# A channel shuffle: fewer, longer tiles, permuted inside one slot

## The chip, the core and the metric

The kernel runs on one core of a Trainium2 chip. The metric is the device time of one execution in microseconds (us); a lower time is better. Engines named here: VectorE (DVE in the profile) copies and rearranges data inside the on-chip memory SBUF; SyncE (SP) and ScalarE (ACT) do nothing here but issue DMAs; 16 DMA engines move data between HBM and SBUF. SBUF has 128 partitions, and sizes "a partition" are bytes in each of them.

## The reference

The input is an image batch of 16 x 64 x 64 pixels with 256 float32 channels each. The channels of every pixel are seen as 8 groups of 32 and are transposed to 32 rows of 8: the output channel j*8 + g is the input channel g*32 + j. No arithmetic is done.

```python
def reference(x, groups):
    batch, h, w, c = x.shape                       # 16, 64, 64, 256
    channels_per_group = c // groups               # 32
    x = x.reshape(batch, h, w, groups, channels_per_group)
    x = x.transpose(0, 1, 2, 4, 3)
    return x.reshape(batch, h, w, c).astype(np.float32)
```

The batch holds 65,536 pixels of 1 KB: 67.11 MB are read and 67.11 MB are written, at least once each.

## The kernel before

The pixels are taken in order. A piece of q pixels a partition is 128 x q consecutive pixels: partition p gets q consecutive pixels, q KB that lie in one run in HBM (`rows`, line 39). `_SLOTS` (line 12) lists the pieces: a first tile with pieces of 4 and 8 pixels, a tile of 28, twelve tiles of 38, and one of 16, together 512 pixels a partition. So there are 16 loads, 16 copies and 16 stores.

Each tile has an input buffer from a pool of two (`in_pool`) and an output buffer from a pool of three (`out_pool`), each as large as the largest tile, 38 KB a partition: 190 KB in all. For every piece three instructions are issued:

- line 55: SP issues the load into the input tile;
- line 57: VectorE copies the piece from the input tile to the output tile, reading with channels in the order (j, g) and writing in one run, which is the permutation;
- line 61: ACT issues the store of the output tile.

The order of instructions on each engine is the program's order (`manual_schedule`), and the waits between engines come from the tiles: a copy waits for its load and for a free output buffer, a store waits for its copy, a load waits until its input buffer has been read by the copy of two tiles before. Loads go through the one queue of SP (q1 in the profile) and stores through the one queue of ACT (q10). Both queues run on the same 16 DMA engines; each DMA of 128 partitions gives every engine eight rows, one packet each.

Of the kernel before, what the change touches and what calls it, by code (L numbers as in the profile page):

```python
# [1 line left out]

# [4 lines left out]


F32 = mybir.dt.float32
P = 128  # L10

_SLOTS = [[4, 8], [28]] + [[38]] * 12 + [[16]]
_IN_BUFS = 2
_OUT_BUFS = 3


@with_exitstack
def kernel(
    ctx: ExitStack,
    tc: tile.TileContext,  # L20
    x: bass.AP,
    groups: bass.AP,
    out: bass.AP,
):
    nc = tc.nc
    b, h, w, c = x.shape
    G = int(groups)
    CPG = c // G
    assert G * CPG == c
    assert sum(map(sum, _SLOTS)) * P == b * h * w  # L30
    biggest = max(map(sum, _SLOTS))

    x_flat = x.rearrange("b h w c -> (b h w c)")
    out_flat = out.rearrange("b h w c -> (b h w c)")

    in_pool = ctx.enter_context(tc.tile_pool(name="in_pool", bufs=_IN_BUFS))
    out_pool = ctx.enter_context(tc.tile_pool(name="out_pool", bufs=_OUT_BUFS))

    def rows(flat, first, q):

        return flat[first * c : (first + P * q) * c].rearrange("(p f) -> p f", p=P)

    ctx.enter_context(tc.manual_schedule(engines=None))
    first = 0
    for parts in _SLOTS:
        in_tile = in_pool.tile([P, biggest * c], F32, name="in_tile")
        out_tile = out_pool.tile([P, biggest * c], F32, name="out_tile")
        at = 0
        pieces = []
        for q in parts:  # L50
            pieces.append((q, first, slice(at * c, (at + q) * c)))
            first += P * q
            at += q
        for q, start, cols in pieces:
            nc.sync.dma_start(out=in_tile[:, cols], in_=rows(x_flat, start, q))  # L55
        for q, start, cols in pieces:
            nc.vector.tensor_copy(  # L57
                out=out_tile[:, cols].rearrange("p (i j g) -> p i j g", j=CPG, g=G),
                in_=in_tile[:, cols].rearrange("p (i g j) -> p i j g", g=G, j=CPG),
            )  # L60
            nc.scalar.dma_start(
                out=rows(out_flat, start, q), in_=out_tile[:, cols]
            )


# [1 line left out]
_INS = ['x', 'groups']  # L67
_OUTS = [((16, 64, 64, 256), 'float32')]

_NUMBERS = {'groups': 8}  # L70


# [26 lines left out]
```

## Time and profile before

| what | value |
|---|---|
| median of 3 runs | 316.04 us (316.04 to 316.05) |
| span of the profiled execution (first to last instruction) | 314.4 us |
| median less that span (no other time of the profiled execution is listed) | 1.6 us |
| DMA, mean over the span | 427 GB/s |
| VectorE busy | 119.0 us, 38%, 16 copies |
| data packets on each of the two queues | 2048, and 256 completions |

The profile is of one execution. Its 40 slices give the busy share of an engine in tenths, for DMA the mean share of the 16 DMA engines. "Chain that ended last" is followed back from the last instruction, step by step, to what released it. In the groups, the number after the bar is the group's busy time, then the mean duration of one instruction in nanoseconds, then the idle time of the engine before them and what ended it. In the windows, the columns are the stretch and its length, the busy time of VectorE and of GpSimd with their instruction counts, a clock that does not matter here, the busy share of the DMA engines and the GB/s that they moved. In a short window this rate is rough, since a packet of 38 KB on each of 16 engines is 0.62 MB.

### The profile page before, as it was taken

Reading aid. Unit: us, or ns where it says so; the run is one execution under the profiler, and the core shown is the slowest. Engines: PE = TensorE matmul, PEld = TensorE weight load, DVE = VectorE, ACT = ScalarE, POOL = GpSimd, SP = SyncE. Lnnn points to the kernel's source line nnn. Section 1 sums busy time; section 2 is a strip of 40 time slices with the busy share of each in tenths; the row PEclk is TensorE's granted clock in tenths of the full one; section 3 lists DMA queues with packets and bytes.
Section 4 is the critical chain, followed back from the end, with each engine's and each line's share of the span. In section 5 each row is a group of like instructions: output and inputs, shape, how many; then the busy total and the mean of one; then the engine's idle time right before and its main releaser. Section 6 shows DMA issues by size and latency. Waiting matters only on the chain.

```text
span 314.4 us, 132 instructions
## 1 busy us (share of the span) xinstructions
DVE 119.0 (38%) x16; POOL 0.2 (0%) x4
## 2 busy tenths in 40 slices
DVE  2081907309109109019028028037046055065400
POOL 0000000000000000000000000000000000000000
DMA  7999999999999999999999999999999999999997
GB/s 317 405 441 416 435 416 483 401 465 406 450 421 446 426 436 436 401 470 396 475 396 475 396 470 401 470 401 470 401 450 421 446 426 436 436 417 450 429 421 321
DMA packets 4608, 134.22 MB, mean 427 GB/s; under 512 B 512, under 2 KB 512, under 8 KB 768
## 3 DMA queue, kind: packets, MB, share of 16 engines
q1 hardware_dynamic: 2304, 67.11, 49.8%
q10 hardware_dynamic: 2304, 67.11, 49.4%
HBM read 67.11 MB, written 67.11 MB: 427 GB/s over the span
## 4 chain that ended last, share of the span: by engine, by line
DMA 76%; DVE 19%; issue 0%; SPq 0%; DVEq 0%
DMA in_tile<-in_x_dram 76%; DVE out_tile L57 19%; SPq L55 0%; DVEq L57 0%
## 5 line engine op out<-in xcount | busy, mean ns | idle before, releaser
L57 DVE COPY out_tile<-in_tile 128x9728 f32<-128x9728 f32 (+4 forms) x16 | 119.0, 7440 | 179.4 <-DMA in_tile<-in_x_dram 179.4
L80 POOL MEMSET const-uint8-127<- 128x1 uint8 x1 | 0.1, 103 | 0.0
L80 POOL MEMSET const-bfloat16-1.0<- 128x1 bf16 x1 | 0.1, 102 | 0.0
L80 POOL MEMSET const-float32-1.0<- 128x1 f32 x1 | 0.1, 100 | 0.0
L80 POOL MEMSET const-float32-0.0<- 128x1 f32 x1 | 0.1, 99 | 0.2 <-issue 0.2
## 6 DMA issues: line engine op xcount, KB each, us to landing
in_tile<-in_x_dram SPq DMA_DIRECT2D x12, 4864.0 KB, 37.0
out_dram<-out_tile ACTq DMA_DIRECT2D x12, 4864.0 KB, 42.6
in_tile<-in_x_dram SPq DMA_DIRECT2D x1, 3584.0 KB, 14.7
out_dram<-out_tile ACTq DMA_DIRECT2D x1, 3584.0 KB, 30.9
in_tile<-in_x_dram SPq DMA_DIRECT2D x1, 2048.0 KB, 30.4
out_dram<-out_tile ACTq DMA_DIRECT2D x1, 2048.0 KB, 15.2
in_tile<-in_x_dram SPq DMA_DIRECT2D x1, 1024.0 KB, 5.4
out_dram<-out_tile ACTq DMA_DIRECT2D x1, 1024.0 KB, 25.0
```

Source lines behind the costliest of these rows:

```text
L57: nc.vector.tensor_copy(out=out_tile[:, cols].rearrange("p (i j g) -> p i j g", j=CPG, g=G), in_=in_tile[:, cols].rearrange("p (i g j) -> ...
L80: nc = _bacc.Bacc("TRN2", target_bir_lowering=False, num_devices=1)
```

## The change

The twelve tiles become eleven of 43 pixels a partition and one of 39. There is one pool of four slots in place of the two pools, and a slot has room for 43 + 8 pixels, 51 KB a partition, 204 KB in all. A load puts its q pixels eight pixels (`_SHIFT`) above the place from which they will be stored. VectorE then permutes them inside the slot, eight pixels at a time, each piece written eight pixels below where it was read, so that a piece overwrites pixels that the piece before it has already read and moved. A tile of 43 takes six copies, the last of 3 pixels; the tile of 39 takes five, the last of 7: 71 copies in all. The store takes the lower q pixels of the slot and follows all of its tile's copies. A load now waits until the store of four tiles before has read the slot. There are 12 loads and 12 stores.

```diff
-_SLOTS = [[4, 8], [28]] + [[38]] * 12 + [[16]]
-_IN_BUFS = 2
-_OUT_BUFS = 3
+_SLOTS = [[43]] * 11 + [[39]]
+_BUFS = 4
+
+_SHIFT = 8
...
-    biggest = max(map(sum, _SLOTS))
+    room = max(map(sum, _SLOTS)) + _SHIFT
...
-    in_pool = ctx.enter_context(tc.tile_pool(name="in_pool", bufs=_IN_BUFS))
-    out_pool = ctx.enter_context(tc.tile_pool(name="out_pool", bufs=_OUT_BUFS))
+    pool = ctx.enter_context(tc.tile_pool(name="pool", bufs=_BUFS))
...
-        in_tile = in_pool.tile([P, biggest * c], F32, name="in_tile")
-        out_tile = out_pool.tile([P, biggest * c], F32, name="out_tile")
+        slot = pool.tile([P, room * c], F32, name="slot")
...
-            pieces.append((q, first, slice(at * c, (at + q) * c)))
+            pieces.append((q, first, at))
...
-        for q, start, cols in pieces:
-            nc.sync.dma_start(out=in_tile[:, cols], in_=rows(x_flat, start, q))
-        for q, start, cols in pieces:
-            nc.vector.tensor_copy(
-                out=out_tile[:, cols].rearrange("p (i j g) -> p i j g", j=CPG, g=G),
-                in_=in_tile[:, cols].rearrange("p (i g j) -> p i j g", g=G, j=CPG),
+        for q, start, at in pieces:
+            nc.sync.dma_start(
+                out=slot[:, (at + _SHIFT) * c : (at + _SHIFT + q) * c],
+                in_=rows(x_flat, start, q),
             )
+        for q, start, at in pieces:
+            for lo in range(at, at + q, _SHIFT):
+                n = min(_SHIFT, at + q - lo)
+                src = slot[:, (lo + _SHIFT) * c : (lo + _SHIFT + n) * c]
+                dst = slot[:, lo * c : (lo + n) * c]
+                nc.vector.tensor_copy(
+                    out=dst.rearrange("p (i j g) -> p i j g", j=CPG, g=G),
+                    in_=src.rearrange("p (i g j) -> p i j g", g=G, j=CPG),
+                )
             nc.scalar.dma_start(
-                out=rows(out_flat, start, q), in_=out_tile[:, cols]
+                out=rows(out_flat, start, q), in_=slot[:, at * c : (at + q) * c]
             )
```

## The prediction

> **What bounds the kernel now.** I read the page's busy times and 40 slices first, then the chain of waits, the groups with shapes kept apart, the waits of SP's queue, the windows, and last the trace's packet records (start, duration, queue and size of each DMA packet).
>
> ```profile
> span 314.4 us, 132 instructions
> ...
> DVE 119.0 (38%) x16; POOL 0.2 (0%) x4
> ...
> DMA  7999999999999999999999999999999999999997
> ...
> q1 hardware_dynamic: 2304, 67.11, 49.8%
> q10 hardware_dynamic: 2304, 67.11, 49.4%
> HBM read 67.11 MB, written 67.11 MB: 427 GB/s over the span
> ## 4 chain that ended last, share of the span: by engine, by line
> DMA 76%; DVE 19%; issue 0%; SPq 0%; DVEq 0%
> ```
>
> The 16 DMA engines are full in every slice but the first and the last: the two queues' shares add to 99.2%. The 19% of VectorE in the chain must not be read as a cost: the chain goes load, copy, load, but while it goes through a copy the store queue keeps the same 16 engines full.
>
> ```profile
> 0.00:2.00 2.00, 0.00 (x0) 0.20 (x4) 1.00 0.18 23
> ...
> 9.00:29.00 20.00, 6.57 (x1) 0.00 (x0) 1.00 1.00 423
> ...
> 60.00:260.00 200.00, 75.15 (x9) 0.00 (x0) 1.00 1.00 433
> ...
> 313.28:314.44 1.16, 0.00 (x0) 0.00 (x0) 1.00 0.00 0
> ```
>
> Last column GB/s: 23 in the first 2 us (the first packet starts at 1.75), 433 in the long mixed stage, 423 from 9 to 29 us, where loads take most of the turns, nothing in the last 1.16 us. VectorE's prices and what SP waits for:
>
> ```profile
> L57 DVE COPY out_tile<-in_tile 128x9728 f32<-128x9728 f32 x12 | 105.5, 8791 | 158.5 <-DMA in_tile<-in_x_dram 158.5
> ...
> L57 DVE COPY out_tile<-in_tile 128x2048 f32<-128x2048 f32 x1 | 2.0, 2019 | 1.5 <-DMA in_tile<-in_x_dram 1.5
> L57 DVE COPY out_tile<-in_tile 128x1024 f32<-128x1024 f32 x1 | 1.1, 1092 | 4.1 <-DMA in_tile<-in_x_dram 4.1
> ```
> ```profile
> SPq L55 <- DMA in_tile<-in_x_dram: 151.2, 13, 13.8
> SPq L55 <- DVE out_tile L57: 106.2, 13, 8.9
> ```
>
> SP is two loads ahead at most and waits for VectorE's copy before the next; a load takes 37 us to land, so its queue holds work meanwhile.
>
> **The time as a sum.** The packet records show one row of one tile per packet, eight rows per DMA and engine. Usual durations: 4096 B 159 ns, 8192 B 309, 16384 B 611, 28672 B 1062, 38912 B 1439. The slope is (1439 - 159)/(38912 - 4096) = 0.03676 ns a byte, and about 8 ns stay over. Each engine moves 134.22/16 = 8.389 MB: 308.41 us. In the mixed stage, with packet bytes spread evenly over their durations, the rate is 433.5 GB/s, so packets of 38912 B follow each other every 38912 x 16/433.5 = 1436.2 ns, 5.6 ns above their 1430.6 of bytes: the fixed cost of a packet, the completions' share in it. There are 256 data packets an engine (32 DMAs of eight): 1.43 us. The first packet starts at 1.75 us and the last ends at 313.28 us, a stretch of 311.53. So 311.53 - 308.41 - 1.43 = 1.69 us are lost otherwise. The records place most of it; an excess is what packets took above the usual for their size, summed and divided by 16:
>
> ```
> excess per engine        us     what runs there
> before 3 us              0.29   first packets, up to 679 ns instead of 159
> 3 to 32 us               0.52   loads alone, then loads with small stores
> 32.9 us                  0.36   one load packet on each engine, 1794 instead of 1439
> after that               0.02   equal loads and stores, then stores alone
> ```
>
> The remaining 0.50 is latency before the first bytes and the engines' spread at the end (their last completions lie 0.4 us apart). Stores alone, 294.5 to 307 us, run at 433.5 GB/s, as fast as the mix. Loads alone do not: 417 GB/s from 3 to 9 us. The stretch is one profiled execution of 314.44 us span; the median of the runs is 316.04, 1.60 more, which I carry over unchanged.
>
> **The change part by part.** *Fewer, longer packets.* 12 loads and 12 stores are 24 x 8 = 192 packets an engine, 64 fewer: 64 x 5.6 ns = 0.36 us saved. Bytes are the same. A 44032 B packet should take 44032 x 0.03676 + 8 = 1627 ns. The Trainium skill's "DMA: Bandwidth & Descriptors" (section "Why small descriptors are slow (HBM only)") gives some three cycles per packet; at 850 MHz, the clock in its port figure, an estimate of 64 x 3.5 = 0.23 us, less than the trace's price.
>
> *The first store.* Now the first tile is 4 KB a partition, copied at 4.06 us, with its first store packet at 9.12. After: the tile lands at about 1.75 + 0.5 + 8 x 1.66 = 15.5, VectorE starts 0.4 later as now. Six pieces: five of 2048 elements at 2.02 and one of 768 at about 0.86 (the 1024 row, 0.9 ns an element), with some 0.06 between them: 11.3 us, to 27.2. Now the first store packet comes 4.0 us after its issue (5.19), that is three load packets of 1.06 and 0.9; with packets of 1.63 it is 5.8. So stores begin at about 33 us, and loads are alone from 3 to 33: 30 us instead of 6, and the load-heavy 9 to 32 us go. The DMA engines are never idle in it: four loads are issued at once, 4 x 13.1 = 52 us of work.
>
> *What loads alone cost* (L). Rows, as excess over the usual packet: 8192 B alone 1.9% (3 to 6 us), 28672 B alone 5.3% (6 to 9 us), both together 3.4%; 38912 B with small stores in between 2.1% (19 to 29 us). Bounds: 1% (half of the least row, for a row pitch that spreads better) and 8% (the one worst microsecond, 8 to 9 us, 399 GB/s against 433.5), so 0.3 to 2.4 us. I take 3% of 30 us, 0.9 us, between the row nearest in packet size (2.1%) and the one nearest in kind (3.4%). It replaces the 0.52 of before. The 0.36 at 32.9 us comes once while packet sizes change; I let it go, and keep it as part of the range.
>
> A rule speaks against the change here: the same page ("Where 436 GB/s comes from") has HBM limit transfers to and from SBUF to about 358 GB/s a core; 30 us at that rate would lose 5.2 us and give about 320. The trace disagrees: loads alone ran at 417.
>
> *SP's wait.* A load now waits for the store of four tiles before, where it waited for a copy. Behind it in SP's queue stand only later loads; VectorE would wait for them. When stores begin, loads are (33 - 2.3)/13.26 = 2.3 tiles ahead, and both queues then take equal turns, as in the mixed stage (loads 215.6, stores 217.9 GB/s). When store k ends, loads stand at k + 3.3 of k + 4 issued: 0.7 tile, some 18 us, still queued against 1 to 2 us until a new load's packets come. Cost nothing; cover 18 us.
>
> *VectorE in the slot.* 71 copies instead of 16: 11 x 11.3 + 10.2 = 134 us instead of 119, in 12 rounds of 26 us each. Hidden by the DMA of other slots; without cover each tile would cost its 11.3. A piece writes where the piece before it read, on one engine in order. No row shows copies inside one tile; below, no gain is possible as VectorE is not waited for by DMA; above, even 4 us a piece (double) is 24 us a tile, still under 26.
>
> *The end.* The last store now is 16 rows, ready 9.6 us before its turn (copy ends 298.4, first packet 307.99). After, when the last load's packets end, stores stand at 11.91 - 2.3 = 9.6 tiles: 0.4 + 1 tiles alone, 18 us, before the last store's turn. Its copies need 0.4 + 10.2 + 0.9 = 11.5 us: 6.5 us to spare. Stores alone run at the full rate, so nothing is lost. After the last packet 1.16 us remain as now.
>
> **Sum.** 308.41 + 192 x 5.6 ns = 1.08, + 0.29 + 0.50 at the ends, + 0.9: 311.18 against 311.53, 0.35 us less. 316.04 - 0.35 = 315.7 us. The 0.2% that a measurement can tell from no change is 0.63 us here, so this is no change.
>
> **Rivals.** *Loads alone cost 2% or less.* The sum then is 310.28 + L with L below 0.62: more than 0.63 us saved. For it: the row nearest in size, 2.1%. Against it: 5.3% with 28672 B alone. Its time is 314.8 (L = 0, the floor) to 315.4; at 1.5% it is 315.2. *Loads alone cost over 6.3%*, 1.89 us, a rate under 406 GB/s, from which the change is slower by more than 0.2%: one mechanism, the read side of HBM in the first 33 us. For it: 399 GB/s at 8 to 9 us and the rows' rise from 1.9 to 5.3%. Against it: 421 to 425 in later single microseconds of nothing but long loads. At 8% it is 2.4 us: 317.2. *VectorE becomes the bound at the end.* If the pieces wait for each other and a tile of 39 takes over 17 us instead of 10, the last store is late and each further microsecond counts in full; at 4 us a piece (19 to 20 us) it adds 3: 318.7. Against it: gaps of copies now are only from waiting for loads. *The change does nothing at all to DMA's order*: equal packets in both queues and full engines, the loads-alone cost as small as the packets' gain; that is my forecast's own case.
>
> **How the numbers follow.** Forecast (L from 2.1 to 6.3%) 0.50, with its own range 315.4 to 316.7; cheaper loads 0.27; costlier loads 0.17; VectorE at the end 0.03; something unseen that slows, such as long rows in the largest slots, 0.03. Faster 0.27, same 0.50, slower 0.23. The range goes from 315.0 (L = 0.2) to 317.0 (L = 2.2): below and above it about 0.08 each.
>
> **What would show it.** Slices of DMA at 9 throughout; the first store packet at about 33 us; a rate of about 420 GB/s before it, 433 to 434 after; 44032 B packets at 1627 ns in the mix; loads never missing from their queue; VectorE about 134 us with idle time for loads only; the last store's packets following the one before without a gap. The prediction is wrong if the rate before the first store is under 406 or near 433, if the load queue runs dry, if pieces take far over 2.02 us, or if the mixed rate of the longer rows is not that of 38912 B.

## The result and the profile after

The changed kernel takes 319.31 us (median of 6 runs, 317.49 to 321.16), against 316.08 for the kernel before in the same session. The ratio is 1.010, 95% interval 1.0066 to 1.0134: 1% slower, where no change (315.7, range 315.0 to 317.0) was forecast. The runs also scatter: 3.7 us between the fastest and the slowest, against 0.5 us before. The profiled run took 320.60 us with a span of 318.8, so 1.8 us lie outside the span. Ratios, here and below, leave out runs over 1.5% above the fastest of their kernel; only the two kernels with three slots had such runs, two of ten and one of ten.

The page of the changed kernel, its busy engines, slices, queues and chain:

```profile
span 318.8 us, 168 instructions
...
DVE 138.7 (44%) x71; POOL 0.2 (0%) x4
...
DMA  8999999999999999999999999999999999999895
...
q1 hardware_dynamic: 1728, 67.11, 49.4%
q10 hardware_dynamic: 1728, 67.11, 48.8%
q14 instruction: 1, 0.01, 0.0%
HBM read 67.11 MB, written 67.11 MB: 421 GB/s over the span
## 4 chain that ended last, share of the span: by engine, by line
DMA 68%; DVE 18%; another core or an unknown queue 9%; issue 0%; SPq 0%; DVEq 0%
```

DMA is still the bound, but the mean rate is 421 GB/s instead of 427, the third slice from the end reads 8, and there is one transfer of instructions in the run that the kernel before did not have. Its windows (columns as before, the last is GB/s):

```profile
5.00:29.00 24.00, 11.55 (x6) 0.00 (x0) 1.00 1.01 438
29.00:36.00 7.00, 6.04 (x3) 0.00 (x0) 1.00 0.90 315
60.00:260.00 200.00, 88.09 (x46) 0.00 (x0) 1.00 1.00 432
...
300.00:304.00 4.00, 3.16 (x1) 0.00 (x0) 1.00 0.36 154
304.00:318.00 14.00, 0.00 (x0) 0.00 (x0) 1.00 0.86 368
```

Loads alone, from 5 to 29 us, lose nothing (with packets spread over their durations the rate is 433.7 GB/s). The loss sits at the first stores, 29 to 36 us, and in the last 18 us. The groups of VectorE, by shape, and SP's waits:

```profile
L64 DVE COPY slot<-slot 128x2048 f32<-128x2048 f32 x59 | 119.5, 2025 | 164.0 <-DMA slot<-in_x_dram 162.4
L64 DVE COPY slot<-slot 128x768 f32<-128x768 f32 x11 | 16.0, 1458 | 0.4
L64 DVE COPY slot<-slot 128x1792 f32<-128x1792 f32 x1 | 3.2, 3200 | 0.0
```
```profile
SPq L55 <- DMA out_dram<-slot: 238.6, 8, 57.6
SPq L101 <- DMA out_dram<-slot: 73.4, 3, 48.8
```

VectorE's pieces cost what was expected where they have eight pixels, and nearly twice that where they have 3 or 7.

**Where the time went: 16 engines, not one.** Every load and store completes once on each of the 16 DMA engines, and the trace records each of these completions. How far the first lies from the last tells how far the engines have drifted apart. From the completion packets (first and last engine, us):

```
                 before                  changed
load, first      3.43 to 3.67  (0.24)    15.46 to 16.51  (1.05)
load, third      15.57 to 15.97 (0.41)   52.31 to 54.90  (2.59)
load, middle     139.3 to 139.8 (0.43)   156.26 to 159.72 (3.46)
load, last       293.62 to 294.04 (0.43) 285.04 to 291.26 (6.22)
store, last but one  307.98 to 308.41    301.28 to 305.88 (4.60)
```

Packets were also followed engine by engine, each packet starting where another ended. In the kernel before, all 16 engines load at the same moment and store at the same moment, turn by turn. In the changed kernel 11 to 12 engines do so and four do the opposite. The break is at the first stores: on most engines the load packet at 31.9 us took 2.6 to 2.9 us instead of 1.63; others got their first store packet one packet earlier and had their slow load, 3.1 to 3.3 us, after it, so that they came out 2 us behind and in the opposite turn. From there almost all the excess, 1 to 3 us each as far as packets can be followed, is on four or five engines, while most of the others have none.

The engines in step had finished the last store but one at 301.28 us. With eight packets of 1.48 us to go they would have ended at 313.1; the forecast's stretch ends at 1.75 + 311.18 = 312.9. So for them the forecast's time held, partly by luck: the 0.9 us for loads alone did not come, and losses that the forecast did not have came in its place (below). The kernel ended at 317.68, on engines that were 4.6 us behind. The others waited for work from 301 to 304 us, because the last load was complete only when its slowest engine was, at 291.3, and 11.4 us of copies followed.

### The profile page after: what moved, and what is told of

Read it like the earlier page. It is cut to its first block, busy times and chain, and to the rows that moved or that the text cites. A ratio compares the mean times of both kernels' runs of the same rounds, so it can differ in the third digit from the quotient of the medians.

```text
span 318.8 us, 168 instructions
## 1 busy us (share of the span) xinstructions
DVE 138.7 (44%) x71; POOL 0.2 (0%) x4
## 4 chain that ended last, share of the span: by engine, by line
DMA 68%; DVE 18%; another core or an unknown queue 9%; issue 0%; SPq 0%; DVEq 0%
DMA slot<-in_x_dram 39%; DMA out_dram<-slot 28%; DVE slot L64 18%; SPq L55 0%; DVEq L64 0%
## 5 line engine op out<-in xcount | busy, mean ns | idle before, releaser
L64 DVE COPY slot<-slot 128x2048 f32<-128x2048 f32 (+1 forms) x71 | 138.7, 1954 | 164.5 <-DMA slot<-in_x_dram 162.4
```

Source lines behind the costliest of these rows:

```text
L64: nc.vector.tensor_copy(out=dst.rearrange("p (i j g) -> p i j g", j=CPG, g=G), in_=src.rearrange("p (i g j) -> p i j g", g=G, j=CPG),)
```

## The experiments

The table is of the profiled runs, from the packet records. "Excess" is what packets took above the usual for their size, per engine; the spread is that of one load's completions. Times in us.

```
kernel               first store  excess 4-60  excess 60-260  spread mid, last
before                    9.1        0.85          0.03         0.43  0.43
changed                  32.1        1.25          0.79         3.46  6.22
small first tiles         9.5        0.98          0.06         0.41  1.19
split last tile          31.9        0.89          2.83         2.67  4.83
old tiles, 68 copies      9.2        0.78          0.06         0.42  0.90
old tiles, 43 copies      9.2        1.03          0.02         0.40  0.40
no copies                21.5        1.23          0.00         0.98  0.99
no copies, nudged        24.3        0.36          0.40         4.79  4.79
three slots               9.2        0.95          0.10         1.88  2.04
twelve of 40             29.9        0.97          0.21         4.18  4.83
two pools, of 40         29.3        3.28         17.78         8.43 19.42
two pools, small+40       9.2        0.86          0.00         0.40  0.45
early small store         9.4        0.81          0.31         0.55  2.40
two pools, late store    27.8        1.43          0.73         3.16  3.81
small pieces, one tile    9.2        0.72          0.06         0.48  0.96
nudged in mid-run        21.5        1.22          3.36         7.78 10.69
long rows, three slots    9.7        1.16          0.50         5.74  7.46
```

**A small start, all else as changed.**

```diff
-_SLOTS = [[43]] * 11 + [[39]]
+_SLOTS = [[4, 8], [31]] + [[43]] * 10 + [[39]]
```

> The changed kernel with its first 43 pixels cut into tiles of 4 + 8 and 31, so that stores begin early; all else as changed. In the changed kernel the completions of one load lie 1.0 us apart among the DMA engines at the first load, 2.6 us after stores begin at 32 us, and 6.2 us at the last; before, never over 0.5 us. Theory A (the long first packets and the late first store put the engines out of step, and they stay so): the spread stays under 1 us, the packets' excess falls from 2.9 us an engine to under 1.2, and the time is 315.5 to 316.5. Theory B (rows of 43 KB collide in HBM whatever comes first): the spread grows past 3 us as in the changed kernel, 318 to 320. Theory C (copies inside the slot disturb the DMAs): as B.

317.03 us (316.76 to 317.32), 1.0021 times before (1.0012 to 1.0031). The engines keep step at 0.41 us until 200 us, and the excess after 60 us is 0.06 instead of 0.79. So rows of 43 KB and copies inside the slot run at the full mixed rate when the start is small; B and C fall as causes of the drift in the changed kernel. (The edit makes both the first packets shorter and the first store earlier; later runs take these apart.) The time is 0.5 us above what A gave: one engine falls 0.5 us behind at 198 us (below) and ends 1.2 us after the first.

**The last tile in two pieces.**

```diff
+_SLOTS = [[43]] * 11 + [[23, 16]]
```

> The changed kernel with its last 39 pixels loaded, copied and stored as 23 and 16. In the profile of the changed kernel DMA ran at 247 GB/s from 300 to 304 us, waiting for the last tile's copies. Theory D (the end alone makes it slower): that hole closes, 1.5 to 2 us less, 317.5 to 318.5 in runs like the profiled one. Theory A and B (the engines are out of step and lose time in the whole span): the hole closes too, but the last engine still ends over 1.5 us after the first, and the time stays over 316.8.

320.90 us (320.29 to 321.65), 1.0142 (1.0119 to 1.0165). In its windows the hole is closed and the time is no better:

```profile
300.00:304.00 4.00, 0.00 (x0) 0.00 (x0) 1.00 1.03 443
...
315.00:319.00 4.00, 0.00 (x0) 0.00 (x0) 1.00 0.23 98
```

From 315 us only a few engines still work. The hole was idle time of engines that were not the last; D falls. The excess after 60 us, 2.83 us an engine here, shows how much it varies from kernel to kernel once the step is lost. It could have hidden a gain, but in the changed kernel itself the engines that ended last had no pause: 305.88 + 8 x 1.48 is 317.7.

**The old tiles in the new slots.**

```diff
+_SLOTS = [[4, 8], [28]] + [[38]] * 12 + [[16]]
```

> The four slots and the copies inside them, with the tiles of before (4 + 8, 28, twelve of 38, 16). Theory A: as before the change, spread under 0.5 us, 315.9 to 316.3. Theory B: the same, 315.9 to 316.3. Theory C: the spread grows past 2 us although rows and start are those of before, 317 to 320.

316.65 us (all but one run 316.61 to 316.79), 1.0014 (1.0004 to 1.0024). Four slots and copies in place cost 0.4 us, not 3: C falls again. The engines stay within 0.45 us until 237 us, then one is 0.9 behind to the end. At 237.0 us the trace has the instruction transfer, 8192 B, on that page as

```profile
q14 instruction: 1, 0.01, 0.0%
```

**No copies at all.**

```diff
-            for lo in range(at, at + q, _SHIFT):
-                ...
-                nc.vector.tensor_copy(...)
             nc.scalar.dma_start(
-                out=rows(out_flat, start, q), in_=slot[:, at * c : (at + q) * c]
+                out=rows(out_flat, start, q),
+                in_=slot[:, (at + _SHIFT) * c : (at + _SHIFT + q) * c],
```

> The changed kernel without VectorE's copies: each tile is stored from where it was loaded, so the output is the input unpermuted. The stores then begin at some 20 us instead of 32, and no store waits for VectorE at the end. Theory C: spread under 1 us and 315 to 316. Theories A and B: excess of 1.5 us or more and a spread of over 2 us remain; without the hole at the end 316.5 to 318.

317.00 us (316.57 to 317.79), 1.0022 (1.001 to 1.0034). The loss at the first stores is there without VectorE, 1.2 us an engine at 16 to 21 us, but it fell on all engines alike: the spread stayed at 0.9 to 1.0 us, and of the packets between 60 and 270 us only one took more than 0.03 us over the usual (0.11). Neither theory had this: the loss at the first stores and the loss of step are two things.

**Pushing four engines out of step, without copies.**

```diff
+    extra = side.tile([P, 32 * c], F32, name="extra")
...
+    nc.sync.dma_start(out=extra[:4, :], in_=rows(x_flat, 0, 32)[:4, :])
     first = 0
```

> The kernel without copies again (rows of 43 KB, no permutation), with one more load first: 32 KB into each of 4 partitions of a tile that nobody reads, which gives four of the 16 DMA engines one more packet of about 1.2 us and so puts them nearly one packet out of step with the others. Without it the completions of one load lay 0.9 to 1.0 us apart from the first load to the last and packets had no excess after the first stores. Theory A2 (engines that are a packet out of step lose time by themselves, some loading while others store): the spread starts at 2 us and grows past 3, and packets between 60 and 260 us get an excess of over 0.3 us an engine, over 1 us on the four. Theory C2 (it takes the copies of VectorE beside engines that are out of step): the spread stays at 2.0 to 2.3 us to the end and the excess between 60 and 260 us stays under 0.05; the time is that of the kernel without copies plus up to 1.2: 317.5 to 318.3.

320.88 us (320.63 to 321.25), 1.015 (1.0135 to 1.0165). The spread went from 1.6 us at the first load and 3.2 at the second to 4.8, with 0.40 us of new excess an engine between 60 and 260 us. Followed packet by packet, nearly all of it is in load packets of four engines, 1.5 to 1.7 us each, and these are the four that carried the extra load; the other twelve have 0.1 us at most. No copy runs in this kernel, so C2 falls and A2 is supported. And at its first store, at 24.3 us, no load packet took over 0.1 us too long: the loss at the first stores did not come here. It is not a clean nudge: the slots lack the eight spare pixels of the kernel above, and the extra load slowed the first packets of all engines, 2.8 us an engine before 4 us against 0.75, which is part of why the time is that long.

**The same nudge in the middle of the run** (the extra load behind the sixth).

```diff
+        if number == 5:
+            nc.sync.dma_start(out=extra[:4, :], in_=rows(x_flat, 0, 32)[:4, :])
```

> Rows of 43 KB without copies, and the 32 KB for four engines now queued behind the sixth load, at some 145 us, when the mixed stage runs without any excess and the completions lie 0.9 to 1.0 us apart. Theory A2 (engines a packet out of step lose time by themselves): spread 1.0 before it, 2.0 to 2.3 just after it, over 2.8 at the end, with new excess in packets after 150 us; 318 to 320. Theory C2: it stays at 2.0 to 2.3 and no excess comes; the time is that without the extra load plus up to 1.2: 317.0 to 318.2.

325.19 us (324.21 to 326.03), 1.0276 (1.0241 to 1.0311). This did not do what it was meant to. At 145 us every engine, not four, had one load packet of up to 4.25 us instead of 1.63. After it the spread was 7.8 us and grew to 10.7, as A2 says, but a stall of all engines came first that neither theory has, and it stays unexplained.

**Twelve tiles of 40 pixels in the slots.**

```diff
+_SLOTS = [[40]] * 12 + [[32]]
```

> The changed kernel with twelve tiles of 40 pixels and one of 32 instead of eleven of 43 and one of 39: the long first load and the late first stores stay, the rows are 7% shorter, and every copy is of 8 pixels. Theory A (the start puts the engines out of step, and that alone decides): the first stores at 30 us cost over 0.8 us an engine again, the spread passes 1.5 us there and grows, 317.3 to 320.5. Theory B (rows of 43 KB are the cause): spread under 1 us, 315.9 to 316.6. The copies of 7 and 3 pixels, which took 3.2 and 1.46 us where 1.79 and 0.86 were expected, are gone; if these mattered the time falls by 1.4 us at most.

319.59 us (318.31 to 321.47), 1.0113 (1.0075 to 1.0151). As A has it: 0.97 us at the first stores, the spread 1.4 us at the first load, 2.2 after the first stores, 4.8 at the end. Row length and odd pieces are not what slows the changed kernel.

**The same list of 40 in the two pools of before.** Only the tile list of the kernel before is changed.

```diff
-_SLOTS = [[4, 8], [28]] + [[38]] * 12 + [[16]]
+_SLOTS = [[40]] * 12 + [[32]]
```

> The kernel before (two input and three output buffers, one copy a tile) with only the tile list changed, to twelve of 40 and one of 32, as they were in four slots at 318.3 to 321.5 us. Theory A (the long first load and the late first store put the engines out of step): the first stores cost over 0.8 us an engine, the spread of a load's completions passes 1.5 us and grows, 317 to 321, with 13 copies and nothing in place. Rival (the slots, with copies in place and many instructions, are the cause): spread under 1.1 us, packets without excess after 60 us, 315.9 to 316.8.

357.17 us (357.11 to 357.42), 1.1288 (1.1266 to 1.131). Far more than any theory had, and with no slots, no copies in place and 13 copies in all. The rate falls in the whole run; the slices of its page and its mixed stage:

```profile
GB/s 360 410 424 387 406 387 406 378 410 387 406 383 387 415 383 401 401 378 415 383 406 392 373 415 383 410 387 401 401 383 378 415 353 414 414 283 433 54 309 195
```
```profile
60.00:260.00 200.00, 69.74 (x8) 0.00 (x0) 1.00 1.00 395
```

DMA's share is 1.00 at 395 GB/s: the engines are busy all the time, but packets take longer. Store packets were 287 ns over their usual 1514 on average between 60 and 270 us; load packets 13 ns over. At most moments some engines load and some store. In the four slots the same list took 319.59 us, so the start does not set the size of the loss by itself; why the two pools make it twelve times as large is open.

**Two pools, the same rows of 40, with the small start kept.**

```diff
+_SLOTS = [[4, 8], [28]] + [[40]] * 11 + [[32]]
```

> The kernel before with its small first tiles kept (4 + 8, 28) and then eleven tiles of 40 and one of 32 in the two pools: 15 loads instead of 16, 16 packets an engine fewer, 0.09 us by the packet price. If a small start is all it takes to keep the engines in step: 315.9 to 316.1, spread 0.45. If rows of 40 KB and more fall out of step by themselves: over 316.8.

316.93 us (316.10 to 318.42), 1.0018 (0.9998 to 1.0037): no difference from before clear of noise, but outside the 315.9 to 316.1 expected of a small start, and by its median over the 316.8 set for rows that fall out of step by themselves. Five of its ten runs are over 317; of the kernel before, three of 19 in the same session. Only one run has a trace. In that one, of 316.29 us, the engines stay within 0.45 us and the mixed stage is back:

```profile
60.00:260.00 200.00, 73.94 (x8) 0.00 (x0) 1.00 1.00 433
```

The two kernels differ only in how the first 40 pixels are cut, 40 us apart. So in these pools the start decides whether the step is lost early, and once lost it is not found again. That rows of 40 KB lose it more readily later in the run is not excluded: the five slower runs have no trace.

**Long rows or a late store?** Three kernels; the first two are edits of the changed one.

```diff
+_SLOTS = [[4, 39]] + [[43]] * 10 + [[39]]
```

> The changed kernel with its first tile in two pieces, 4 and 39 pixels, so that the first load and the first store have rows of 4 KB and the first store starts at some 9 us; every other row is as changed. Without copies, long rows and a first store at 21.5 us cost 1.2 us an engine there, so the copies aren't needed for that loss. Theory G (the length of the row in the first packets and the first store makes the loss and the unequal start): loss under 0.3 us at the first packets and under 0.6 at the first stores, spread 0.45 us for over half the span, 316.6 to 317.3, as with 4 + 8 and 31. Theory H (the lateness of the first store makes it): the same here, so that the next run tells.

318.21 us (317.84 to 319.05), 1.0072 (1.0055 to 1.0089). The changed kernel's rows with an early small store: 0.39 us instead of 1.25 at the first long stores, spread 0.45 to 0.7 us up to 190 us, as G has it; then single engines lose 0.1 to 0.6 us at a time and it ends at 2.4. That is 1.1 us better than the changed kernel, but 1.2 us worse than with 4 + 8 and 31, which G does not explain. The edit also leaves a pause: behind the small store no store ran from 20.4 to 33.4 us, so the first long stores again followed 13 us of loads alone.

```diff
+_SLOTS = [[4, 8, 28]] + [[38]] * 12 + [[16]]
...
+        for q, start, at in pieces:
             nc.scalar.dma_start(
```

> The tiles of before in four slots with the first 40 pixels as one tile of three pieces (4, 8, 28) that are all copied before the first of them is stored: rows of 4 KB come first in both queues, but the first store starts at some 26 us, after a stretch of loads alone, as in the changed kernel. Theory G (row length): the first stores cost under 0.5 us an engine, the spread stays at 0.45 us, 316.5 to 317.0. Theory H (lateness): they cost 0.8 us or more, the spread passes 1.2 us and grows, 317.3 to 320.

316.73 us (316.66 to 316.79), 1.0015 (1.0006 to 1.0024). The first store started at 9.2 us all the same, since a store waits for its own copy only: the test was void, and the kernel behaved as the old tiles in slots, now with the first 40 pixels as one tile. The next one makes it late, in the kernel before:

```diff
+_SLOTS = [[4, 8, 28]] + [[38]] * 12 + [[16]]
...
-        for q, start, cols in pieces:
+        for q, start, cols in reversed(pieces):
             nc.vector.tensor_copy(
...
+        for q, start, cols in pieces:
             nc.scalar.dma_start(
```

> The kernel before with its first 40 pixels as one tile of three pieces that VectorE copies in reverse order, so that the piece with rows of 4 KB is stored first but only when all three are copied, at some 26 us; all later tiles are those of before. (In the run before this the first store was not late after all, since each store waits for its own copy only.) Theory G (the long rows of the first packets and the first store make the loss): under 0.5 us at the first stores, spread 0.45 us to the end, 316.0 to 316.5. Theory H (the late first store makes it): 0.8 us or more there, spread over 1.2 us and growing, 317 and more; in these two pools twelve tiles of 40 with a long and late start took 357 us.

319.95 us (318.70 to 321.43), 1.0123 (1.0084 to 1.0162). Its windows:

```profile
6.00:24.00 18.00, 8.85 (x3) 0.00 (x0) 1.00 1.00 434
25.00:28.00 3.00, 1.33 (x1) 0.00 (x0) 1.00 0.79 243
60.00:260.00 200.00, 79.12 (x9) 0.00 (x0) 1.00 1.00 433
```

With rows of 4 KB first, the first stores at 27.8 us cost 0.67 us an engine and the first long ones another 0.6 at 50 to 56 us; the spread goes from 0.59 us to 1.95 and 3.8. This is the kernel before with its first 40 pixels as one tile and in another order, and it is as slow as the changed kernel. H is supported: long rows first and copies in place are not needed. The edit has a side effect, since one tile takes one buffer for all three pieces, and VectorE then had to wait for output buffers:

```profile
DVE out_tile L57 <- DMA out_dram<-out_tile: 28.4, 2, 26.0
```

Around the longer of its two waits the loads paused too, from 74 to 88 us. The step had gone before it, though: the load that ended at 55 us already had a spread of 1.95 us. Nor is a late first store always enough: without copies it came at 21.5 us, and the engines stayed within 1 us. Whether the copies or the longer stretch makes that difference no run shows.

The same windows show what loads alone cost: 434 GB/s from 6 to 24 us, with the rows of 28 and 38 KB that the kernel before loads there too. From 6 to 9 us its packets of 28 KB took under 0.1% over the usual, where the prediction's row has 5.3% for the kernel before. There the first store had been issued at 5.19 us, here none until 24.75; VectorE's copies ran from 15.15 us without effect.

**The instruction transfer, and few copies.**

```diff
 _SLOTS = [[4, 8], [28]] + [[38]] * 12 + [[16]]
-_SHIFT = 8
+_SHIFT = 13
```

> The tiles of before in four slots, copied thirteen pixels at a time instead of eight: 43 copies instead of 68. Theory F (the 0.4 us that the 68 copies cost came from the fetch of further instructions, 8 KB on one DMA engine): no fetch in the run, spread 0.45 us to the end, 316.05 to 316.3. Rival (the slots cost it): 316.5 to 316.8 without a fetch. With three slots the engines fell out of step in most runs, which I put down to a load queue that ran dry; with four it should not.

316.41 us (316.30 to 317.30), 1.0003 (0.9992 to 1.0013). Its page has no transfer of instructions, and the spread is 0.40 us from the first load to the last, where 68 copies had 0.45, then 0.9 right after the transfer. F is supported; what it costs is 0.2 to 0.4 us, because the kernel ends with the engine that carried it. Its groups also show the price of odd pieces:

```profile
L64 DVE COPY slot<-slot 128x3328 f32<-128x3328 f32 x27 | 156.8, 5806 | 98.5 <-DMA slot<-in_x_dram 98.1
L64 DVE COPY slot<-slot 128x3072 f32<-128x3072 f32 x12 | 35.5, 2956 | 0.4
```

13 pixels cost 1.74 ns an element, 12 pixels 0.96.

**Three slots with still fewer copies**, the old tiles twenty pixels at a time, and long rows twenty-two at a time.

```diff
+_SLOTS = [[4, 8], [28]] + [[38]] * 12 + [[16]]
+_BUFS = 3
+_SHIFT = 20
```

> The tiles of before copied inside three slots of 58 KB, twenty pixels at a time: 29 copies instead of the 68 that the same tiles take with eight at a time in four slots. That kernel with 68 copies was 0.4 to 0.5 us slower than before; its trace had one DMA of 8 KB of instructions at 237 us, after which one DMA engine was 0.5 us behind to the end. Theory F (the fetch of VectorE's further instructions costs it): no such DMA in the run, spread 0.43 us to the end, 316.05 to 316.25. Rival (the slots themselves, their place in SBUF or the load waiting for a store, cost it): 316.5 to 316.8 without any fetch.

317.80 us (316.17 to 321.33), 1.0035 (1.0018 to 1.0052). No instruction transfer, as F has it, and the best runs are those of before; but most are over 317, and in the profiled one, of 317.84 us, the engines lose step, to 1.9 us by the middle. I took the load queue with three slots to run dry. The trace agrees: from 29.8 to 34.9 us no engine had a load packet, where the same tiles in four slots never had such a pause of over 2.5 us, and the spread of the loads after it went from 0.45 us to 0.71, 1.38 and 1.87. No run tests the pause apart.

```diff
+_SLOTS = [[4, 8], [32]] + [[44]] * 10 + [[28]]
+_BUFS = 3
+_SHIFT = 22
```

> Long rows with the small first tiles of before: 4 + 8, 32, ten tiles of 44 and one of 28 in three slots of 66 KB, copied 22 pixels at a time (28 copies). If a small start keeps the engines in step and few copies need no further instructions: spread 0.45 us to the end, 28 x 8 = 224 packets an engine against 256, 0.18 us less than before: 315.9 to 316.1. If rows of 43 KB and more cost something of their own: 316.5 to 317.1, as with the small first tiles and eight pixels at a time (317.0).

318.69 us (316.43 to 321.88), 1.0074 (1.0051 to 1.0096). It misses both forecasts. The trace is of the slowest run, and has the same pause, 33.2 to 38.3 us without a load, after which the spread went from 0.64 us to 2.85. So with three slots a small start does not keep the step.

No variant was faster than the kernel before by more than the noise.

## Why the prediction was wrong

**Right.** *The bound* is DMA, and the packets' arithmetic held: 44032 B packets took 1627 ns, as worked out, and the engines in step were on their way to 313.1 us against 312.9. *The first store* came at 32.05 us (33 forecast) after 27 us of loads alone, and *SP's wait* was hidden: DVE's idle time is all for loads, and the load queue never held up the engines. *The mixed rate* from 60 to 260 us was 433.4 to 433.7 GB/s where all engines were in step.

**Wrong: "What loads alone cost (L)".** I took 3% of 30 us, 0.9 us, from short stretches at the start of the kernel before. It was nothing: 433.7 GB/s from 5 to 29 us. The excess rows that I scaled up were not the price of loads: with a late first store the same 28 KB rows, loaded alone, had next to none (under 0.1% against 5.3%), which points to the beginning of the stores. The rule of the Trainium skill's "DMA: Bandwidth & Descriptors", section "Where 436 GB/s comes from", that HBM limits such transfers to about 358 GB/s a core, is contradicted again, now by 433.7 GB/s over 24 us; that the time it gave, about 320, lies near the measured one is chance. The two losses that I did not foresee are the first packets (0.77 us an engine instead of 0.29) and the first stores (1.25 us). The event at 32.9 us of the kernel before, 0.36 us, which I "let go", was this second loss in small: 0.4 to 0.5 us lie just before the first store with long rows in the kernels with the old tiles, with small first tiles and with the early small store too.

**Wrong, and the step that decided: "0.50 at the ends", with the sum made for one engine.** I saw that the last completions lay 0.4 us apart and carried that over as a constant. It is a result of the start. With the late first store some engines fell into the opposite turn, their packets then took 1 to 3 us longer over the run, and the kernel ends with the last engine, 4.6 us behind the rest at the last store but one, where 0.50 us had been put for both ends. The pair with rows of 40 KB in two pools (357 against 317 us) and the kernel before with a late first store (320) show the late start as the cause apart from the slots, the copies in place and the row length; the kernel without copies, with a first store at 21.5 us and the step kept, shows that it is not enough in every kernel.

**The rivals.** "VectorE becomes the bound at the end" named a wait that did arise, the last store late and the engines idle from 301 to 304 us, but with the hole closed the time did not fall. "Loads alone cost over 6.3%" ended on the right side for a reason that did not exist. None had the engines apart.

**"VectorE in the slot"** was mis-sized by a little: a tile takes 11.75 us instead of 11.3, the last 11.4 instead of 10.2, because a piece of 3 pixels takes 1.46 us and one of 7 takes 3.20 (0.86 and 1.79 expected). The Trainium skill's "VectorE: DVE Perf Modes", section "Mode 2×_2P — use both read ports for one tensor", says that the doubled mode needs an outermost dimension that is even, or odd and the same in source and destination. The source here has the pixels as outermost dimension; the destination is written in one run. The rows agree as far as even and odd go: 8 and 12 pixels near 0.97 ns an element, 3, 7 and 13 at 1.74 to 1.90. No run shows whether an odd number that is the same on both sides would have kept the lower price. It does not decide the time. A price of 71 copies that I did not have is the 8 KB of instructions that one DMA engine carried: 0.2 to 0.4 us, again through the engine that ends last.

**Open.** Why engines in opposite turns lose time: in kernels whose engines mostly share a direction (on average 5 to 7% of them in the lesser one) packets after 60 us were 0 to 0.6 ns over the usual, and with 11 to 35% in it mostly 2 to 150 ns over, but the amount does not follow the share (29%: 2 ns; 22%: 151 ns), and the kernel without copies had none at 10%. That reads and writes of HBM get in each other's way is an idea that no run here tests. Why the first stores stall the engines at all, why they did not in the nudged kernel, why the two pools with rows of 40 lose twelve times what the slots lose, and why an early small store did not keep the step to the end with 39 and 43 pixels behind it, is open too.

## What to carry to other kernels

A DMA-bound kernel at 99% busy is 16 engines that end separately; read the completions of one transfer engine by engine before carrying a tail over as a constant, because a load is complete, and the kernel done, only with the slowest. Start both queues early and with small rows: in the two pools, the first 40 pixels cut as 4 + 8 + 28 or as one tile made 317 or 357 us with all else equal; in the slots a small start was worth 2.3 us. Longer transfers were to save a few nanoseconds a packet here, and a long first one cost the start; and an odd number of rows in a strided copy nearly doubled its price.

## What the runs showed of the hardware

- All 16 engines took turns between the two queues in unison for 300 us (a load's completions within 0.51 us); once a load's completions were more than 1.5 us apart, they came back within half a microsecond in no kernel.
- The first stores after 20 to 30 us of loads alone cost 0.7 to 1.25 us an engine in seven kernels, with or without copies, in the changed kernel as one load packet of 2.6 to 3.3 us instead of 1.63 just before them. In the nudged kernel they cost nothing. One further load of 32 KB on four engines in mid-run stalled all 16 for up to 2.6 us.
- In the kernels with 64 to 71 copies a packet of 8192 B of instructions ran at 198 to 237 us, in none with 43 or fewer. In two of them, whose engines were in step until then, one engine was 0.5 us late from there on.
- The Trainium skill's "DMA: Bandwidth & Descriptors", section "Why a DMA increments its semaphore by 16 and not by 1", says that a transfer's engines finish independently and each posts its own completion. The trace agrees, with the sixteen completions of one load up to 19.4 us apart in the kernel of 357 us.
